# A long convolution's second transform step: from three rounded products on the whole array to fp32 products on its quarters

## The chip, the core and the metric

The kernel runs on one core of one Trainium2 chip. The metric is the device time of one execution in microseconds (us), and less is better. TensorE is PE in the profile, its weight loads are PEld, VectorE is DVE, ScalarE is ACT, GpSimd is POOL, and SP is SyncE, which here only issues DMAs.

## What is computed

One encoder block over 2048 tokens of 1024 channels, all in fp32. Cut to what matters:

```python
u = rmsnorm(x, norm_g);  p = einsum('bld,de->ble', u, w_in)          # 56 column blocks of 128
c_val, c_gate, c_z, hy_p, hy_z = split(p)
a = depthwise_conv(c_val * sigmoid(c_gate), 31 taps); a = silu(group_layernorm(a)) * silu(c_z)
x0, x1, v = split(depthwise_conv(hy_p, 3 taps))
k = filters(2L long)                                                  # a small MLP of positions
y = irfft(rfft(v * x1, 2L) * rfft(k, 2L), 2L)[:L] + (v * x1) * skip
y = group_rmsnorm(y * x0) * silu(hy_z)
out = rmsnorm(x + einsum('blm,md->bld', concat([a, y]), w_out), final_g)
```

## The kernel before

The program has five stretches. First the input's norm and some projections (0 to 100 us of the span) and the filters. Then, to 1500 us, the in-projections, with the convolution's taps on DVE beside them; each group of 128 channels of `a` is stored to the DRAM tensor `MX`, and the first step of the Fourier transform (`stage1`) stores signal and filter spectra to `AU` and `AK`. Third comes the **pair stage** (1500 to 1830 us), which the change rewrites. The last is the **epilogue** (to the end): for each of 16 blocks of 128 tokens `before` transforms back (products `Y`, transposes `T`, sums `vp`, rows `R`) and norms, and `after` multiplies by the second half of `w_out`. Between the two lies the **hand-over**.

The transform's second step works on 32 pairs of frequencies. A pair has 128 rows (2 frequencies, real and imaginary part, 32 places) of 1024 channels. Four products with 128x128 matrices `g` are needed: the signal's spectrum (`forward`), the filter's real and imaginary part (`product`, tiles `kr` and `ki`), and the way back (`inverse`). The two frequencies don't mix, so half of each matrix is zero. TensorE takes fp32r operands, which are rounded, in one instruction for 512 columns. To keep fp32's accuracy `parts` splits every operand on ACT and DVE into a rounded and a rest part, and `three` (L835 to L838) makes three products of them for each half of the channels. In every fifth pair (`DUP`) `product` makes one product less and copies instead.

`conf_step` is the first half of the out-projection, which needs `MX` alone: 16 blocks in two halves each, a half being 8 steps of 3 products (L781 to L783). 16 steps stand ahead of the pair stage, 176 are handed out within it (`some`, `CF`), the last 64 come behind it (`for _ in conf`). The Tile scheduler is free to order every engine's instructions. Tile `o` has one PSUM bank. `wo_split` (L490, L491) scales and splits the second half of `w_out`, into the tiles of the first, once `conf` is done with them.

`fetched` loads a block's gates `x0` and `hz` and the rows `v` (`long<-VD`) that `inverse` has stored to `VD`; a block's `v` has rows of all 32 pairs.

Of the kernel before, what the change touches and what calls it, by code (L numbers as in the profile page):

```python
# [18 lines left out]
P = 128  # L19
L = 2048  # L20
# [13 lines left out]
PITCH = (N2 + 1) * D  # L34
TWO_PI_INV = float(np.float32(1.0 / (2.0 * math.pi)))
# [9 lines left out]
DUP = 5  # L45
CF0 = 16
CF = 176
# [20 lines left out]
def _constants():  # L68
# [28 lines left out]
    st2 = np.zeros((NPAIR, P, 8, P), f32)  # L97
    n2 = np.arange(N2)[:, None]
    k2 = np.arange(N2)[None, :]
    for p in range(NPAIR):  # L100
        m = np.zeros((2, 2, N2, 2, 2, N2))
        for l in range(2):
            kk = l * 32 + p
            g = np.exp(-1j * np.pi * ((2 * kk + 1) * n2 / 4096.0 + k2 * n2 / 16.0))
            m[0, l, :, 0, l, :] = g.real
            m[1, l, :, 0, l, :] = -g.imag
            m[0, l, :, 1, l, :] = g.imag
            m[1, l, :, 1, l, :] = g.real
        m = m.transpose(2, 0, 1, 3, 4, 5).reshape(P, P)
        re, im = m[:, :64], m[:, 64:]  # L110
        for j, x in enumerate((m, m.T, np.concatenate([re, re], axis=1), np.concatenate([-im, im], axis=1))):
            st2[p, :, 2 * j], st2[p, :, 2 * j + 1] = _split(np.ascontiguousarray(x).astype(f32))
# [58 lines left out]
def hybrid_kernel(ctx: ExitStack, tc: tile.TileContext, A, out):  # L171
# [10 lines left out]
    MX = dram.tile([NG, P, L], F32, name="MX")  # L182
# [315 lines left out]
    with ExitStack() as c0:  # L498
# [78 lines left out]
        def conf_tail(i, acc, r, some):  # L577
# [12 lines left out]
            nc.sync.dma_start(MX[i], acc)  # L590
# [150 lines left out]
        def mixed(i, pool, bufs=1):  # L741

            mr = pool.tile([P, KT, P], F32, name="mr", bufs=bufs)
            nc.sync.dma_start(mr, MX[:, :, i * P:(i + 1) * P].rearrange("k p t -> p k t"))
            mh = pool.tile([P, KT, P], F32R, name="mh")
            nc.scalar.activation(mh, mr, AF.Copy)
            ml = pool.tile([P, KT, P], F32R, name="ml")
# [42 lines left out]
    pso = ctx.enter_context(tc.tile_pool(name="psO", bufs=1, space=PSUM, reuse_waits="tile"))  # L790
# [29 lines left out]

    def conf_to(n):

        while held[0] < min(n, 2 * KT * (L // P)):
            next(conf)

    with ExitStack() as c0:
# [8 lines left out]
        def three(o, g, j, hi, lo, cs):  # L835
            mm(o, g[:, j], hi[:, cs], start=True, stop=False)
            mm(o, g[:, j], lo[:, cs], start=False, stop=False)
            mm(o, g[:, j + 1], hi[:, cs], start=False, stop=True)  # L838

        seen = [0]  # L840

        def some():
            seen[0] += 1
            conf_to(CF0 + CF * seen[0] // (6 * NPAIR))

        HALF = [slice(c * TC, (c + 1) * TC) for c in range(2)]

        def load_pair(p):
            g = f1.tile([P, 8, P], F32R, name="g", bufs=4)
            nc.gpsimd.dma_start(g, A["c_st2"][p])  # L850
# [3 lines left out]
            nc.sync.dma_start(ak, gather(AK, p))  # L854
            return g, au, ak

        def parts(x, name, bufs, pool):
            if pool is None:
                both = long(F32R)
                h, l = both[:, :D], both[:, D:]  # L860
            else:
                h, l = (pool.tile([P, D], F32R, name=name + w, bufs=bufs) for w in "hl")
            nc.scalar.activation(h, x, AF.Copy)
            nc.vector.tensor_sub(l, x, h.bitcast(F32))
# [195 lines left out]
```

## Time and profile before

| what | value |
|---|---|
| median of 3 runs | 2160.95 us (2158.88 to 2162.77) |
| the profiled execution | 2159.41 us, its span 2157.7 us |
| PE busy | 2076.8 us, 96% of the span |
| DVE, ACT busy | 1581.6 us (73%), 1127.2 us (52%) |
| granted TensorE clock, mean | 0.99 |

Shares are means over the whole span. A matmul's duration in the trace holds its way through the array, so consecutive ones overlap; what one costs in a row of many is the distance between their starts. A `x` count in a row of the trace counts instructions; an fp32 product of TensorE is two of them, an fp32r product is one.

### The profile page before, as it was taken

The page shows a single profiled execution, that of the slowest core. Times are in us where ns is not written, and L with a number is a line of the kernel's source. Part 1 is how long each engine was busy: PE and PEld are TensorE (multiplying, and loading weights), DVE is VectorE, ACT ScalarE, POOL GpSimd, SP SyncE. Part 2 cuts the span into 40 slices and gives each one's busy share as a digit, 9 for nine tenths or more (in the row PEclk, how much of TensorE's full clock was granted, in tenths as well). Part 3 has the DMA queues.
Part 4 walks back from the last instruction along what each step waited for, and adds up shares of the span by engine and source line. Part 5 has one row for each costly group of instructions (what it writes and reads, how often), then busy time and mean ns, then how long its engine had stood idle before and what let it go on. Part 6 is the DMA issues. An engine that isn't in the chain of part 4 may idle for free. (4 is left out here: it accounts for less than half of the span.)

```text
span 2157.7 us, 23506 instructions
## 1 busy us (share of the span) xinstructions
PE 2076.8 (96%) x9076; PEld 1617.5 (75%) x9076; DVE 1581.6 (73%) x1519; ACT 1127.2 (52%) x1663; POOL 25.3 (1%) x52
## 2 busy tenths in 40 slices
PE   6999999999999999999999999999999999999998
PEld 5677788887887887877878878777777776666666
DVE  5687639498597695994994976986787886375664
ACT  6488712333434433433344344447898997365662
POOL 0000000000000000000000000001000000000000
PEclk9999999999999999999999999999999999999999
DMA  8433311112112202212121121127877786776652
GB/s 311 157 116 147 140 37 52 67 59 74 45 69 78 78 25 74 78 35 92 60 67 51 65 77 54 59 79 251 298 267 259 262 277 229 254 205 185 186 159 66
DMA packets 157104, 277.34 MB, mean 129 GB/s; under 512 B 11062, under 2 KB 93366, under 8 KB 151872
## 3 DMA queue, kind: packets, MB, share of 16 engines
q1 hardware_dynamic: 151008, 253.82, 35.8%
q0 software_dynamic: 5984, 22.02, 3.3%
q8 instruction: 71, 1.16, 0.2%
q14 instruction: 41, 0.34, 0.0%
HBM read 175.14 MB, written 100.66 MB: 128 GB/s over the span
## 5 line engine op out<-in xcount | busy, mean ns | idle before, releaser
L235 PE MATMUL mm<-uh,wh 128*128 128x512 f32 x1792 | 709.8, 397 | 6.8 <-ACT wh L226 3.5
L236 PE MATMUL mm<-ul,wh 128*128 128x512 f32 x1792 | 705.4, 394 | 1.6 <-DVE ul L296 1.6
L237 PE MATMUL mm<-uh,wl 128*128 128x512 f32 x1792 | 705.4, 394 | 0.3 <-DVE wl L228 0.3
L541 DVE SCALAR_TENSOR_TENSOR long<-apad,small,long 128x2048 f32<-128x2048 f32 x240 | 562.7, 2344 | 9.2 <-ACT long L538 6.7
L235 PEld LDWEIGHTS mm<-uh,wh 128*128 128x128 f32 x1792 | 340.3, 190 | 88.9 <-DVE apad L533 5.9
L236 PEld LDWEIGHTS mm<-ul,wh 128*128 128x128 f32 x1792 | 340.2, 190 | 77.7 <-DVE ul L296 3.6
L237 PEld LDWEIGHTS mm<-uh,wl 128*128 128x128 f32 x1792 | 339.8, 190 | 74.8 <-issue 1.6
L608 ACT ACTIVATE ppad<-mm 128x512 f32<-128x512 f32 x96 | 57.3, 597 | 224.6 <-PE mm L237 203.0
L783 PE MATMUL o<-wo,ml 128*128 128x512 f32 x384 | 152.2, 396 | 0.0
L781 PE MATMUL o<-wo,mh 128*128 128x512 f32 x384 | 152.0, 396 | 0.0
L782 PE MATMUL o<-wo,mh 128*128 128x512 f32 x384 | 151.9, 396 | 0.0
L226 ACT ACTIVATE wh<-wr 128x1024 fp32r<-128x1024 f32 x56 | 59.3, 1060 | 154.7 <-PE mm L236 147.4
L533 DVE TENSOR_TENSOR apad<-mm,apad 128x512 f32<-128x512 f32 x32 | 22.1, 692 | 154.7 <-PE mm L237 154.7
L228 DVE TENSOR_TENSOR wl<-wr,wh 128x1024 fp32r<-128x1024 f32 x56 | 68.3, 1220 | 53.7 <-ACT wh L226 52.7
L664 ACT ACTIVATE t<-aux 64x512 fp32r<-64x512 f32 x64 | 37.8, 594 | 103.5 <-PE aux L662 103.5
L782 PEld LDWEIGHTS o<-wo,mh 128*128 128x128 f32 x384 | 72.2, 188 | 18.9 <-issue 3.3
L783 PEld LDWEIGHTS o<-wo,ml 128*128 128x128 f32 x384 | 72.2, 188 | 18.1 <-issue 2.9
L781 PEld LDWEIGHTS o<-wo,mh 128*128 128x128 f32 x384 | 72.2, 188 | 17.0 <-issue 1.2
L564 ACT ACTIVATE long<-aux 128x512 f32<-128x512 f32 x32 | 19.0, 594 | 101.3 <-PE aux L563 101.3
L619 ACT ACTIVATE long<-ppad,small 128x512 f32<-128x512 f32 x64 | 68.8, 1076 | 1.9
L621 DVE SCALAR_TENSOR_TENSOR long<-ppad,small,long 128x512 f32<-128x512 f32 x64 | 66.8, 1046 | 0.7 <-ACT long L619 0.5
L681 ACT ACTIVATE t<-aux 128x512 f32<-128x512 f32 x64 | 37.7, 590 | 55.6 <-PE aux L679 55.4
(217 smaller groups left out, 3116.8 us busy)
## 6 DMA issues: line engine op xcount, KB each, us to landing
wr<-in_w_in_dram SPq DMA_DIRECT2D x56, 512.0 KB, 3.6
AK<-ak SPq DMA_DIRECT2D x64, 256.0 KB, 2.0
AU<-t SPq DMA_DIRECT2D x64, 256.0 KB, 2.3
au<-AU SPq DMA_DIRECT2D x32, 512.0 KB, 4.6
g<-in_c_st_dram POOLq DMA_DIRECT2D x32, 512.0 KB, 5.9
ak<-AK SPq DMA_DIRECT2D x32, 512.0 KB, 5.3
VD<-vs SPq DMA_DIRECT2D x32, 512.0 KB, 5.3
long<-VD SPq DMA_DIRECT2D x16, 1024.0 KB, 5.3
```

The lines of the kernel that those rows point to most:

```text
L226: nc.scalar.activation(wh, wr, AF.Copy)
L228: nc.vector.tensor_sub(wl, wr, wh.bitcast(F32))
L235: mm(pt, wh[:, k], uh[t][:, k], start=(k == 0), stop=False)
L236: mm(pt, wh[:, k], ul[t][:, k], start=False, stop=False)
L237: mm(pt, wl[:, k], uh[t][:, k], start=False, stop=(k == KT - 1))
L541: nc.vector.scalar_tensor_tensor(acc, apad[:, j:j + L], sm("dw_w", i * CK + j), acc, op0=OP.mult, op1=OP.add)
L608: nc.scalar.activation(ppad[:, 1 + t * TC:1 + (t + 1) * TC], pt, AF.Copy)
L619: nc.scalar.activation(co, v(ppad[:, a + 1:a + 1 + n]), AF.Identity, bias=sm("sh_b", j), scale=sm("sh_w", 3 * j + 1))
L621: nc.vector.scalar_tensor_tensor(co, v(ppad[:, a:a + n]), sm("sh_w", 3 * j), co, op0=OP.mult, op1=OP.add)
L781: mm(o, mh[:, k], wh[:, cs], start=(k == 0), stop=False)
L782: mm(o, mh[:, k], wl[:, cs], start=False, stop=False)
L783: mm(o, ml[:, k], wh[:, cs], start=False, stop=(k == KT - 1))
```

## The change

The 128x128 matrices become 64x64 ones without the zero blocks, in fp32 and unsplit. `quads` makes one of the four products of a pair: four `mm` calls, one for each frequency and each half of the channels, each on 64 rows and 64 columns of the array, that is on a quarter; the two row halves write different halves (PSUM banks) of the output tile. `parts` and the `DUP` branch go. ACT copies the spectrum out in one 128x1024 piece and swaps real and imaginary rows by four copies of 32 rows. `g` becomes 128x288 and is loaded by SP instead of POOL; `au`, `ak` and `vs` move in two DMAs of 64 rows each.

PE and SP now follow the program's order in the pair stage (`manual_schedule`): all four products of a round stand together, then 7 or 8 steps of `conf`. A block of `conf` is loaded and split one block ahead (`prepare`), and `o` has two banks. 8 steps of `conf` stand ahead of the stage and 8 behind the last `inverse`. `MX` is laid out by blocks of tokens, so that its load has 4 KB in a row and its store 512 B. Four row blocks of `w_out` and the first block's gates are loaded within the stage, and the first `wo_split` writes a tile of its own. `xr<-PT` moves from SP to POOL.

```diff
+KR, UU, KI, BACK = 0, N2, 3 * N2, 5 * N2
+NG2 = BACK + P
-DUP = 5
-CF0 = 16
-CF = 176
+CF0 = 8
+CF7 = 14
+CFY = 6
...
-    MX = dram.tile([NG, P, L], F32, name="MX")
+    MX = dram.tile([L // P, P, NG, P], F32, name="MX")
...
-            nc.sync.dma_start(MX[i], acc)
+            nc.sync.dma_start(MX[:, :, i].rearrange("b p t -> p b t"), acc.rearrange("p (b t) -> p b t", t=P))
...
-            nc.sync.dma_start(mr, MX[:, :, i * P:(i + 1) * P].rearrange("k p t -> p k t"))
-            mh = pool.tile([P, KT, P], F32R, name="mh")
+            nc.sync.dma_start(mr, MX[i])
+            mh = pool.tile([P, KT, P], F32R, name="mh", bufs=bufs)
...
-    pso = ctx.enter_context(tc.tile_pool(name="psO", bufs=1, space=PSUM, reuse_waits="tile"))
+    pso = ctx.enter_context(tc.tile_pool(name="psO", bufs=2, space=PSUM, reuse_waits="tile"))
...
+    def prepare(i):
+        parts = mixed(i, f1, 2) if i else first.pop()
+        xr = row()
+        nc.sync.dma_start(xr, A["x"][i * P:(i + 1) * P])
+        state[i] = (xr, *parts)
-        if c == 0:
-            mh, ml = mixed(i, io, 2) if i else first.pop()
-            xr = row()
-            nc.sync.dma_start(xr, A["x"][i * P:(i + 1) * P])
-            state[i] = (xr, mh, ml)
+        if c == 0 and i + 1 < L // P:
+            prepare(i + 1)
...
-        def gather(src, p):
-            return bass.AP(tensor=src.tensor, offset=src.offset + p * PITCH,
-                           ap=[[D, N2], [32 * PITCH, 4], [1, D]])
-        seen = [0]
-        def some():
-            seen[0] += 1
-            conf_to(CF0 + CF * seen[0] // (6 * NPAIR))
+        def gather(src, p, l):
+            return bass.AP(tensor=src.tensor, offset=src.offset + (32 * l + p) * PITCH,
+                           ap=[[D, N2], [64 * PITCH, 2], [1, D]])
...
-            g = f1.tile([P, 8, P], F32R, name="g", bufs=4)
-            nc.gpsimd.dma_start(g, A["c_st2"][p])
-            au = f1.tile([P, D], F32, name="au", bufs=2)
-            nc.sync.dma_start(au, gather(AU, p))
-            ak = f1.tile([P, D], F32, name="ak", bufs=2)
...
+            g = f1.tile([P, NG2], F32, name="g", bufs=4)
+            nc.sync.dma_start(g, A["c_st2"][p])
+            both = []
+            for name, src, bufs in (("au", AU, 2), ("ak", AK, 3)):
+                x = f1.tile([P, D], F32, name=name, bufs=bufs)
+                for l in range(2):
+                    nc.sync.dma_start(x[rows2(l)], gather(src, p, l))
+                both.append(x)
+            return g, *both
+        def quads(name, bufs, g, at, x, back=False):
+            o = ps.tile([P, D], F32, name=name, bufs=bufs)
+            for l in range(2):
+                for c in range(2):
+                    j = at + 64 * l * back
+                    i, k = (c, l) if back else (l, c)
+                    mm(o[rows2(k), HALF[i]], g[rows2(i), j:j + 64], x[rows2(i), HALF[k]], start=True, stop=True)
+            return o
+        def spectrum(g, au, ak):
             both = long()
             us, uw = both[:, :D], both[:, D:]
...
+            nc.scalar.activation(us, quads("u", 1, g, UU, au), AF.Copy)
+            for q in range(4):
+                nc.scalar.activation(uw[32 * q:32 * (q + 1)], us[32 * (q ^ 1):32 * (q ^ 1) + 32], AF.Copy)
+            return g, us, uw, ak
+        def product(g, us, uw, ak):
+            k = [quads("k", 2, g, at, ak) for at in (KR, KI)]
+            for x, y in zip((us, uw), k):
+                nc.vector.tensor_mul(x, x, y)
+            y = fp.tile([P, D], F32, name="y", bufs=2)
+            nc.vector.tensor_add(y, us, uw)
+            return g, y
...
+            nc.scalar.activation(vs, quads("u", 1, g, BACK, y, back=True), AF.Copy)
+            for l in range(2):
+                nc.sync.dma_start(gather(VD, p, l), vs[rows2(l)])
+        with tc.manual_schedule(engines={mybir.EngineType.PE, mybir.EngineType.SP}):
+            loads = {p: load_pair(p) for p in range(2)}
+            prepare(0)
+            conf_to(CF0)
+            spec = spectrum(*loads.pop(0))
+            y = None
+            for p in range(NPAIR):
+                if p == 0:
+                    done, y = None, product(*spec)
+                    spec = spectrum(*loads.pop(1))
+                    loads[2] = load_pair(2)
+                else:
+                    now = spec
+                    if p + 1 < NPAIR:
+                        spec = spectrum(*loads.pop(p + 1))
+                    done, y = y, product(*now)
+                if p + 3 < NPAIR:
+                    loads[p + 3] = load_pair(p + 3)
+                if done is not None:
+                    inverse(p - 1, *done)
+                if p == 3:
+                    nc.sync.dma_start(HZ[NG - 1], hz)
+                if p == NPAIR - 4:
+                    for k in range(4):
+                        wo_load(1, k)
+                    ahead = gates(0, io)
+                conf_to(held[0] + (CFY if p == NPAIR - 1 else 7 if p < CF7 else 8))
+            inverse(NPAIR - 1, *y)
+            for _ in conf:
+                pass
+        wo_split(1, 0, io.tile([P, 2 * D], F32R, name="wo0"))
...
+        def fetched(b, ahead=None):
+            x0, hz = ahead or gates(b, ep)
...
-                nc.sync.dma_start(pt[js], src)
+                nc.gpsimd.dma_start(pt[js], src)
...
-        rest = [fetched(0)]
-        for k in range(4):
-            wo_load(1, k)
-        rest.append(fetched(1))
-        for _ in conf:
-            pass
-        for k, make in enumerate([apad_tile, ppad_tile]):
-            wo_split(1, k, make(F32R))
-        for k in range(2, KT):
+        rest = [fetched(0, ahead), fetched(1)]
+        for k in range(1, KT):
             if k >= 4:
                 wo_load(1, k)
-            wo_split(1, k, wo_tile(k))
+            wo_split(1, k, apad_tile(F32R) if k == 1 else ppad_tile(F32R) if k == 2 else wo_tile(k - 1))
```

On PE, in the pair stage (tiles `uv` belong to `forward` or `inverse`), this is a piece of before:

```order
L836 MATMUL kr<-akh,g 128x512
L837 MATMUL kr<-akl,g 128x512
L838 MATMUL kr<-akh,g 128x512
L837 MATMUL uv<-aul,g 128x512
L838 MATMUL uv<-auh,g 128x512
L837 MATMUL uv<-aul,g 128x512
L838 MATMUL uv<-auh,g 128x512
L836 MATMUL uv<-long,g 128x512
L837 MATMUL uv<-long,g 128x512
L838 MATMUL uv<-long,g 128x512
L836 MATMUL ki<-akh,g 128x512
L781 MATMUL o<-apad,mh 128x512
```

and this a whole round of the change, with the ends of the `conf` steps around it:

```order
L788 MATMUL o<-wo_10090,mh 128x512
L789 MATMUL o<-wo_10090,ml 128x512
L875 MATMUL u<-au,g 64x512 x4
L875 MATMUL k<-ak,g 64x512 x8
L875 MATMUL u<-y,g 64x512 x4
L787 MATMUL o<-wo_10125,mh 128x512
L788 MATMUL o<-wo_10125,mh 128x512
```

The sixteen products of a round (`x4`, `x8`, `x4`) stand in one run; the last round's way back, alone, is followed by 24 products of `conf` and then by the epilogue. On ACT two rounds of the change read:

```order
L882 ACTIVATE long<-u 128x1024
L884 ACTIVATE long<-long 32x1024 x2
L752 ACTIVATE mh<-mr 128x1024
L884 ACTIVATE long<-long 32x1024 x2
L897 ACTIVATE vs<-u 128x1024
L882 ACTIVATE long<-u 128x1024
L884 ACTIVATE long<-long 32x1024 x4
L897 ACTIVATE vs<-u 128x1024
```

Tile `u` has one buffer, so the second `u` of a round waits for `long<-u`, and the next round's first for `vs<-u`. On SP the hand-over of before reads (`t` are rows of `w_out`, `x_...` and `hz` gates):

```order
L913 DMA VD<-vs 32x4x1024
L744 DMA mr<-MX 128x8x128
L804 DMA xr<-in_x_dram 128x1024
L952 DMA x_12947<-X_60 128x8x128
L954 DMA hz<-HZ 128x8x128
L956 DMA long<-VD 128x2048
```

and that of the change:

```order
L899 DMA VD<-vs 32x2x1024 x2
L487 DMA t<-in_w_out_dram 128x512
L899 DMA VD<-vs 32x2x1024 x2
L487 DMA t<-in_w_out_dram 128x512 x3
L824 DMA PT<-xr 128x1024
L950 DMA long<-VD 128x2048
```

The gates are gone from ahead of the first `long<-VD`; three loads of `w_out` and the last store of `PT` stand there instead.

## Rows read from the trace of the kernel before

**Rows 1.** The page: busy time by engine; DMA share in 40 slices of the span

```profile
PE 2076.8 (96%) x9076; PEld 1617.5 (75%) x9076; DVE 1581.6 (73%) x1519; ACT 1127.2 (52%) x1663; POOL 25.3 (1%) x52
DMA  8433311112112202212121121127877786776652
```

**Rows 2.** Three stretches; us, busy (instructions) of PE, PEld, DVE, ACT, POOL, clock, DMA, GB/s

```profile
1500.40:1829.30 328.90, 316.99 (x1310) 239.78 (x1308) 255.89 (x239) 283.06 (x412) 14.86 (x28) 1.00 0.79 269
1829.30:1901.70 72.40, 64.81 (x279) 41.90 (x277) 32.82 (x43) 33.63 (x49) 0.00 (x0) 1.00 0.81 259
1901.70:2157.70 256.00, 247.44 (x1134) 169.77 (x1132) 148.16 (x196) 134.09 (x227) 0.00 (x0) 0.99 0.56 154
```

**Rows 3.** Timeline of PE: start, duration; first and last of 23 products in a row

```profile
1838.04 0.39 PE L782 MATMUL o<-apad,mh 128*128 128x512 f32 x1
...
1843.15 0.40 PE L783 MATMUL o<-wo,ml 128*128 128x512 f32 x1
```

**Rows 4.** Line L836, first of `three`, in the pair stage: PE, PEld, clock, DMA, GB/s

```profile
1500.00:1831.00 331.00, 99.45 (x244) 45.48 (x244) 1.00 0.79 268
```

**Rows 5.** Waits of PE in the pair stage: us in total, times, longest

```profile
PE uv L836 <- ACT long L878: 3.8, 12, 0.8
PE kr L836 <- ACT t L892: 2.6, 4, 1.3
```

**Rows 6.** Timeline of PE around four fp32 products on a quarter of the columns each

```profile
419.96 1.07 PE L569 MATMUL vp<-long,ones_g 128*32 128x512 f32 x8
420.96 0.50 PE L235 MATMUL mm<-uh,wh 128*128 128x512 f32 x1
```

**Rows 7.** Timeline of PE around four fp32 products on half of the columns each

```profile
1945.78 0.39 PE L783 MATMUL o<-wo,ml 128*128 128x512 f32 x1
1946.11 1.94 PE L969 MATMUL Y<-long,winv 128*64 128x512 f32 x8
1947.97 0.50 PE L781 MATMUL o<-apad,mh 128*128 128x512 f32 x1
1948.31 0.39 PE L782 MATMUL o<-apad,mh 128*128 128x512 f32 x1
```

**Rows 8.** Weight loads of `Y`: busy us, mean ns of one, idle before

```profile
L969 PEld LDWEIGHTS Y<-long,winv 128*64 128x64 f32 x128 | 8.6, 135 | 14.7 <-issue 11.9 <-ACT y L971 1.1 <-DMA xr<-PT 0.4
```

**Rows 9.** ACT and DVE in the pair stage, by line: busy us, mean ns of one

```profile
L877 ACT ACTIVATE long<-uv 64x512 f32<-64x512 f32 x64 | 38.2, 596 | 1.1
L876 ACT ACTIVATE long<-uv 128x512 f32<-128x512 f32 x64 | 38.1, 595 | 8.5 <-PE uv L838 6.3 <-DVE long L864 0.8
L863 ACT ACTIVATE auh<-au 128x1024 fp32r<-128x1024 f32 x32 | 33.8, 1057 | 8.4 <-PE uv L838 7.8 <-ACT akh L863 0.3
L901 DVE TENSOR_TENSOR long<-long,ki 128x1024 f32<-128x1024 f32 x26 | 31.7, 1220 | 1.1 <-PE ki L838 1.1
```

**Rows 10.** The page's DMA issues: KB each, us from issue to landing

```profile
au<-AU SPq DMA_DIRECT2D x32, 512.0 KB, 4.6
```

**Rows 11.** Timeline of the hand-over, SP's queue and PE: start, duration

```profile
1835.39 3.08 SPq L956 DMA_DIRECT2D long<-VD  x1
1828.99 0.40 PE L838 MATMUL uv<-long,g 128*128 128x512 f32 x1
1845.11 1.07 PE L969 MATMUL Y<-long,winv 128*64 128x512 f32 x2
1901.66 0.78 PE L781 MATMUL o<-apad,mh 128*128 128x512 f32 x1
```

**Rows 12.** Two operations of the epilogue: busy us, mean ns of one

```profile
L986 DVE RECIPROCAL r<-r 128x256 f32<-128x256 f32 x16 | 28.0, 1749 | 2.9 <-ACT r L985 2.7
L996 ACT ACTIVATE mh<-m 128x1024 fp32r<-128x1024 f32 x16 | 16.9, 1053 | 23.9 <-PE o L782 17.3 <-DVE m L994 6.5
```

**Rows 13.** Line L969 in the hand-over, and the clock behind it (columns as in rows 2)

```profile
1845.00:1901.60 56.60, 11.62 (x36) 2.23 (x36) 0.99 0.76 244
1901.00:1905.00 4.00, 3.98 (x15) 2.37 (x15) 3.38 (x5) 2.40 (x4) 0.00 (x0) 0.57 1.04 240
```

More of the change, by code (lines that the diff above doesn't have):

```diff
@@ L95, in _constants @@
     st1 = np.stack([x for m in (s1u, s1k, s1k0) for x in _split(m.astype(f32))], axis=1)
-    st2 = np.zeros((NPAIR, P, 8, P), f32)
+    st2 = np.zeros((NPAIR, P, NG2), f32)
     n2 = np.arange(N2)[:, None]
@@ L100, in _constants @@
     for p in range(NPAIR):
-        m = np.zeros((2, 2, N2, 2, 2, N2))
+        fw = np.zeros((2, N2, 2, 5, N2))
+        bw = np.zeros((2, 2, N2, 2, N2, 2))
         for l in range(2):
@@ L104, in _constants @@
             g = np.exp(-1j * np.pi * ((2 * kk + 1) * n2 / 4096.0 + k2 * n2 / 16.0))
[L105 to L112, printed above, removed]
+            re = np.stack([g.real, -g.imag], axis=1)
+            im = np.stack([g.imag, g.real], axis=1)
+            for b, x in enumerate((re, re, im, -im, im)):
+                fw[l, :, :, b] = x
+            for h in range(2):
+                bw[h, 0, :, l] = re.transpose(2, 0, 1)
+                bw[h, 1, :, l] = im.transpose(2, 0, 1)
+        st2[p] = np.concatenate([fw.reshape(P, 5 * N2), bw.reshape(P, P)], axis=1)
     a = np.pi * (2 * np.arange(64)[:, None] + 1) * np.arange(64)[None, :] / 128.0
@@ L819, in hybrid_kernel, with gates @@
     conf = conf_steps()
+    def gates(b, pool):
+        x0 = pool.tile([P, NG, P], F32, name="x0")
+        nc.sync.dma_start(x0, X0[:, :, b * P:(b + 1) * P].rearrange("k p t -> p k t"))
+        hz = pool.tile([P, NG, P], F32, name="hz")
+        nc.sync.dma_start(hz, HZ[:, :, b * P:(b + 1) * P].rearrange("k p t -> p k t"))
+        return x0, hz
     def conf_to(n):
@@ L829, in hybrid_kernel @@
         ps = c0.enter_context(tc.tile_pool(name="psB", bufs=1, space=PSUM, reuse_waits="tile"))
-        def gather(src, p):
-            return bass.AP(tensor=src.tensor, offset=src.offset + p * PITCH,
-                           ap=[[D, N2], [32 * PITCH, 4], [1, D]])
[L835 to L838, printed above, removed]
@@ L857, in parts @@
[L857 to L864, printed above, removed]
-            return h, l
-        def both_parts(g, au, ak):
-            return g, parts(au, "au", 1, f1), parts(ak, "ak", 2, fp)
@@ L906, in inverse @@
-        def inverse(p, g, yh, yl):
-            vs = fp.tile([P, D], F32, name="vs", bufs=2)
-            for cs in HALF:
-                V = ps.tile([P, TC], F32, name="uv", bufs=3)
-                three(V, g, 2, yh, yl, cs)
-                nc.scalar.activation(vs[:, cs], V, AF.Copy)
-                some()
-            nc.sync.dma_start(gather(VD, p), vs)
-        conf_to(CF0)
-        loads = {p: load_pair(p) for p in range(2)}
-        nc.sync.dma_start(HZ[NG - 1], hz)
-        split = both_parts(*loads.pop(0))
@@ L919, in hybrid_kernel @@
-        spec = forward(*split)
-        split = both_parts(*loads.pop(1))
-        loads[2] = load_pair(2)
-        y = None
-        for p in range(NPAIR):
-            done = y
-            y = product(p, *spec)
-            if p + 1 < NPAIR:
-                spec = forward(*split)
-            if done is not None:
-                inverse(p - 1, *done)
-            if p + 2 < NPAIR:
-                split = both_parts(*loads.pop(p + 2))
-            if p + 3 < NPAIR:
-                loads[p + 3] = load_pair(p + 3)
@@ L934, in hybrid_kernel @@
-        inverse(NPAIR - 1, *y)
+            nc.scalar.activation(us, quads("u", 1, g, UU, au), AF.Copy)
[9 more added lines that the diff above has]
+            return g, y
@@ new lines, in inverse @@
+        def inverse(p, g, y):
+            vs = fp.tile([P, D], F32, name="vs", bufs=2)
+            nc.scalar.activation(vs, quads("u", 1, g, BACK, y, back=True), AF.Copy)
[31 more added lines that the diff above has]
+                pass
@@ L1005, in after @@
             for c, cs in enumerate(halves):
-                o = (ps if c else pso).tile([P, TC], F32, name="o")
+                o = pso.tile([P, TC], F32, name="o")
                 for _ in outproj(o, mh, ml, cs):
```

43 lines of the change are left out of this document (3 added, 40 removed).

## Prediction

> **What bounds the kernel now.** The page comes first [rows 1]: PE is busy 96% of the span, DVE 73%, ACT 52%, and the DMA engines stand at 7 to 8 tenths in the slices of the pair stage. PE therefore sets the time nearly everywhere, and a change pays where it takes work or gaps from PE. The windows show where [rows 2]: from 1500.4 to the last `inverse` at 1829.3 us PE started 1310 instructions; ACT was busy 283 of 329 us there, so it is close behind. What a product of the split kind costs is read from 23 starts in a row [rows 3]: (1843.15 - 1838.04) / 22 = 0.232 us. 1310 of them take 304 us, so 25 us of the 329 are gaps. The longest entries in the list of waits, 3.8 and 2.6 us, are on ACT's copies [rows 5]; most of the rest lies within overlapping durations, where the trace names nobody.
>
> **The products of the transform.** Line L836 ran 244 times in the stage [rows 4], L837 and L838 as often: 3 x 244 = 732 products x 0.232 = 169.8 us. All go. In their place stand 32 rounds of four `quads`, each of four fp32 products of 512 columns on a quarter of the array (32 x 4 x 4 = 512 products, 1024 instructions, so that the page's 9076 become 9368). What one `quads` costs hangs on how many quarters run at once. The trace has two relatives. Four fp32 products on a quarter of the columns each, 8 instructions, take 1.07 us from the first start to the last end, and the next matmul starts 1.00 us after the first [rows 6]: all four ran together, two instructions deep. Four on half of the columns each take 1.94 us, and the next starts 1.86 us after the first [rows 7]: two ran together, four deep. The difference, (1.86 - 1.00) / 2 = 0.43 us, is one such step. So the columns divide freely. That row halves do, no row shows: the nearest are full columns' worth of streams in [rows 6], where four different streams entered the array at once, while here there are two for each row half. Bounds for a `quads`: 2 steps = 0.86 us if the quarters run together, 4 steps = 1.72 if row halves take turns, 8 steps = 3.44 if nothing overlaps. I take 0.86, since rows of both kinds show the array dividing in as many parts as it is given, and the two row halves here write different banks.
>
> Going in and out of such a run costs a little [rows 7]: 0.33 us from the start of the last full product to the first `Y` where 0.232 is usual, 1.86 against 4 x 0.43 = 1.72 within, and 0.34 for the first full product after it: 0.10 + 0.14 + 0.11 = 0.35 us. It is paid once a round, as all sixteen products stand together. A round costs 4 x 0.86 + 0.35 = 3.8 us, 32 rounds 121 us: **49 us less on PE**.
>
> The Trainium skill ("TensorE: Matmul & The Clock Gate", Part 3, "The mechanism" and "What overlaps and what doesn't") says that a weight load overlaps with running matmuls only where the row group differs. Within a round every step needs weights for the same rows as the step before. The loads of `Y` take 135 ns each [rows 8] and are likewise for the same rows, and they did not show: [rows 7] leave 0.14 us over the four steps in all. By the rule each of 8 steps would be 0.135 longer, 8 x 32 x 0.135 = 35 us in all, an estimate; the trace decides for none. The same part ("Measured speedup vs the span model") gives 3.07 for four row tiles side by side in place of 4; by it a `quads` would be 3.44 / 3.07 = 1.12 us and the rounds 33 us longer, an estimate too. Both stand below as one rival, worked out as a mechanism of this kernel.
>
> **The gaps in the stage.** `parts` goes, three splits for each pair, 1.06 us on ACT [rows 9] and 1.22 on DVE each. ACT per round: `long<-u`, four copies of 32 rows and `vs<-u`, each 1024 columns, so about 1.06 us whatever the rows (64 and 128 rows both cost 0.6 for 512 columns in [rows 9]), and half of a split of `mr`: 6.5 x 1.06 = 6.9 us. A round on PE is 3.8 + 24 x 0.232 = 9.4 us, with 21 products 8.7. As `u` has one buffer there is a loop through ACT: first `quads` 0.86 and some 0.3 until ACT starts, `long<-u` 1.06, four copies 4.2, at times `mh` 1.06, `vs<-u` 1.06: 8.5 us at most. It fits, with 0.2 to 0.9 us to spare, and `long<-u` ends 2.3 us into the round, before the third `quads` ends at 2.7. DVE needs 3 x 1.22 + 0.6 + 0.7 = 5 us. Loads are issued two rounds ahead, some 15 us, and land in about 5 [rows 10]. DMA: 32 x (0.15 + 3 x 0.52) + 46 x 0.52 + 4 = 83 MB, which over 300 us is 277 GB/s; [rows 2] have 269 at a share of 0.79. It is tight but has room. I take 6 us of gaps for 25 now, **19 us less**; bounds 0 and 32 (1 us a round).
>
> **The hand-over.** The last `inverse` now starts its last product at 1829.0, `long<-VD` is issued at 1835.4, `Y` starts at 1845.1 and the first product of the epilogue's out-projection at 1901.7 [rows 11]. Between 1829.3 and 1901.7 PE started 279 instructions [rows 2], 36 of them `Y` [rows 13]; some 195 are `conf`. After the change only 24 are left there: 171 are done earlier, within the stage, and cover nothing here. So the last `inverse` comes at 1500.4 + (768 - 24) x 0.232 + 121 + 6 = 1800. From there: `v` must make its way out and in, 1845.1 - 1829.0 = 16 us as before (the gates no longer stand ahead of it, but three loads of `w_out` and a store do). Of these 5.6 are covered by `conf`; the splits of `w_out` on ACT and DVE fall into the rest. Then the chain from `Y` to the first `mh`, an estimate by the pieces' sizes: on PE the four products 1.9 [rows 7] and transposes, sums and `R` some 1.6; on ACT and DVE five pieces of 512 columns at 0.6 to 0.7, 3.2 [rows 9]; four of 256 columns at about 0.45, 1.8; the reciprocal 1.75 and `mh` 1.05 [rows 12]. That is 11.3 us, with a dozen handings-on of 0.1 to 0.2 us 13 to 14. The first out-projection product stands at 1800 + 16 + 14 + 1 = 1831 instead of 1901.7: 71 us earlier. But less of the epilogue is done by then: the program's order has 12 `Y` products, before there were 18 [rows 13], and ten transposes fewer: 3 + 1 + 0.5 = 4.5 us to be made up. PE sits idle for some 10 us on `v`. After the idle stretch ahead of 1901 the granted clock was 0.57 for 4 us [rows 13], that is, mostly 1.2 instead of 2.4 GHz; I add 1.5 us for slow products in the chain. Sum: -71 + 4.5 + 1.5 = **-65 us**. The same by parts: -49 - 19, and +3 for the hand-over.
>
> The epilogue's other edits I cost at nothing: `xr<-PT` on POOL leaves SP's queue, and PE was busy 247 of 256 us there [rows 2], so no load sets its pace. If POOL were late with them, `after` would wait at its add, a block later. The stores of `MX` in 512-byte pieces lie where the DMA share is 1 to 2 tenths [rows 1].
>
> **The number.** The profiled execution took 2159.4 us for a span of 2157.7. 2157.7 - 65 = 2093, with 1.7 around it 2094; the median of the runs is 1.5 above that execution, so 2095 us. 0.2% (4 us) is about what a measurement can tell from no change.
>
> **Rivals.**
> 1. *Row halves take turns.* For: no row shows them together. Against: [rows 6, 7] for columns. A `quads` is 1.72 us, a round 7.2; 32 x 3.44 = 110 us more: 2205 us, slower. It decides from a round of 3.8 + 65 / 32 = 5.8 us on.
> 2. *Something is exposed in each round*: weight loads, 8 x 0.135 = 1.1 us a round [rows 8], or the loop through ACT, if a copy of 32 rows takes 1.3 us (9.5 us for the loop against 8.7 to 9.4, some 0.5 us a round). 16 to 35 us: 2111 to 2130.
> 3. *DMA holds the stage back.* At the 269 GB/s of [rows 2] 83 MB take 309 us, 9 more than I have: 2104. Against: the packets of `MX` are larger now.
> 4. *The hand-over has no cover.* If `v` needs 5 us more behind the loads of `w_out`, and PE's order holds back `Y` or `R`: 2103. If it is quick and the gaps vanish (-6, -8): 2081; with rounds of 3.44 us, 2070.
>
> **Chances.** The forecast with rivals 3 and 4, 2080 to 2112: 0.60. Rival 2, 2112 to 2135: 0.15. Rival 1: 0.13. Quicker than 2080: 0.10. About no change, as a mixture of 1 and 2: 0.02. From 2070 to 2130 holds 0.8. Faster 0.85, the same 0.02, slower 0.13.
>
> **What would show it.** In the timeline of a round: eight groups of four starts 0.43 us apart, 3.8 us from `conf` to `conf`; if row halves take turns, sixteen groups of two. Then PE's waits in the stage: on `u` for ACT none over 0.5 us. The last `inverse` near 1800, `Y` 16 us later, out-projection from 1831, and 262 us from there to the end. I am wrong above all if a round is not 3.8 us, next if `u` waits for ACT.

## The result and the profile after

The changed kernel takes 2091.24 us (median of 4 runs, 2088.11 to 2094.68) against 2160.86 before (4 runs, 2158.88 to 2162.77): a ratio of 0.968, 95% interval 0.966 to 0.970. The forecast was 2095. The profiled execution took 2088.11 us for a span of 2086.3.

The page answers to [rows 1]: PE is still busy 96%, with the 9368 instructions that were counted out. What is new is the DMA row, 9 tenths throughout the pair stage.

```profile
PE 2006.1 (96%) x9368; PEld 1517.2 (73%) x9368; DVE 1468.1 (70%) x1411; ACT 1057.0 (51%) x1455; POOL 24.6 (1%) x52
DMA  8523412121221211212122212122899999877652
```

The windows of the pair stage, the hand-over and the epilogue (columns as in [rows 2]):

```profile
1500.10:1801.60 301.50, 296.58 (x1768) 173.79 (x1766) 154.47 (x144) 218.99 (x210) 0.00 (x0) 0.99 0.96 276
1801.60:1837.50 35.90, 22.00 (x80) 9.24 (x76) 18.05 (x24) 20.34 (x31) 3.07 (x6) 0.81 0.97 278
1837.50:2086.30 248.80, 240.58 (x1165) 169.22 (x1164) 150.42 (x200) 141.36 (x237) 13.23 (x26) 0.99 0.58 170
```

The stage is 27 us shorter although 171 more products of `conf` lie in it, and the hand-over has shrunk: from the last `inverse` to the first out-projection product of the epilogue (1840.2) it is 39 us instead of 72, and from there to the end 246 instead of 256. One round in the timeline of PE (start, duration):

```profile
1603.63 0.40 PE L789 MATMUL o<-wo,ml 128*128 128x512 f32 x1
1603.96 1.09 PE L875 MATMUL u<-au,g 64*64 64x512 f32 x8
1604.87 1.90 PE L875 MATMUL k<-ak,g 64*64 64x512 f32 x16
1606.58 1.04 PE L875 MATMUL u<-y,g 64*64 64x512 f32 x8
1607.55 0.50 PE L787 MATMUL o<-wo,mh 128*128 128x512 f32 x1
1607.89 0.39 PE L788 MATMUL o<-wo,mh 128*128 128x512 f32 x1
```

Read the distances between starts. The 16 instructions of `k` (two `quads`; a step is four instructions, one on each quarter) take 1606.58 - 1604.87 = 1.71 us, four steps of 0.43: all four quarters run at once. From the last `conf` product to the second one after the run it is 4.26 us; less 2 x 0.232 that is 3.80 us for a round's `quads`, the number of the forecast. After the first three, the rounds start 8.67 us apart with 21 products of `conf` (two of them 8.9 and 9.1), and 9.37 with 24, from 1630 to 1780 without exception.

PE's waits from 1490 to 1850 us (total, times, longest):

```profile
PE Y L963 <- DMA long<-VD: 11.9, 3, 7.4
PE u L875 <- ACT long L882: 2.2, 1, 2.2
PE o L787 <- ACT mh L752: 1.8, 1, 1.8
```

Within the stage there are two worth the name: `u` ahead of the first `inverse`, and `o` for `mh` near 1788 us, after which the clock fell to half for 3.4 us. The large one is in the hand-over, which the timeline shows; first SP's queue, then PE:

```profile
1802.97 1.16 SPq L899 DMA_DIRECT2D VD<-vs  x2
1808.76 0.36 SPq L950 DMA_DIRECT2D long<-VD  x1
1811.45 3.30 SPq L950 DMA_DIRECT2D long<-VD  x1
1816.22 9.64 SPq L834 DMA_DIRECT2D hz<-HZ  x1
1825.91 4.64 SPq L950 DMA_DIRECT2D long<-VD  x1
...
1814.95 3.47 PE L963 MATMUL Y<-long,winv 128*64 128x512 f32 x6 [7.39 <-DMA long<-VD]
1825.91 1.94 PE L963 MATMUL Y<-long,winv 128*64 128x512 f32 x2 [3.62 <-DMA long<-VD]
1836.86 1.04 PE L963 MATMUL Y<-long,winv 128*64 128x512 f32 x2 [0.91 <-DMA long<-VD]
1840.21 0.50 PE L787 MATMUL o<-wo,mh 128*128 128x512 f32 x1
```

The first `v` is there 13.8 us after the last product of the last `inverse` has started (1801.2). But in PE's order `Y` of the second and third block stand ahead of the first block's out-projection, and their `v` come late. The second block's was issued at 1811.45 and had landed only when `Y` started at 1825.91. Its packets of 8 KB moved from 1819.1 to 1824.7, after those of the gates issued ahead of it (1813.5 to 1818.2), with the DMA engines full:

```profile
1815.00:1825.90 10.90, 6.22 (x20) 1.90 (x21) 2.61 (x3) 3.29 (x5) 1.17 (x3) 0.81 1.08 286
```

The third block's was issued only at 1825.91, as one issue of `hz<-HZ` held SP's queue for 9.64 us before it. Behind the second block's `Y` stood the last four `vp` instructions of the first block, whose operand ACT had done at 1823.1: they ran at 1827.77. The out-projection starts at 1840.2.

### The profile page after: what moved, and what is told of

It is laid out like the page before. It is cut to its first block, busy times and chain, and to the rows that moved or that the text cites. A ratio compares the mean times of both kernels' runs of the same rounds, so it can differ in the third digit from the quotient of the medians.

```text
span 2086.3 us, 23788 instructions
## 1 busy us (share of the span) xinstructions
PE 2006.1 (96%) x9368; PEld 1517.2 (73%) x9368; DVE 1468.1 (70%) x1411; ACT 1057.0 (51%) x1455; POOL 24.6 (1%) x52
## 4 chain that ended last, share of the span: by engine, by line
PE 73%; DVE 17%; DMA 3%; issue 3%; ACT 3%; SPq 2%; DVEq 0%; ACTq 0%
PE mm L241 14%; PE mm L242 14%; PE mm L243 14%; DVE long L547 7%; PE o L787 5%; PE o L789 5%; PE o L788 5%; PE u L875 2%; PE k L875 2%; DVE long L628 2%; DVE long L627 2%; PE Y L963 1%; DVE t L671 1%; PE op L412 1%; PE op L411 1%
## 5 line engine op out<-in xcount | busy, mean ns | idle before, releaser
L787 PE MATMUL o<-wo,mh 128*128 128x512 f32 x384 | 156.9, 409 | 0.0
L788 PE MATMUL o<-wo,mh 128*128 128x512 f32 x384 | 151.6, 395 | 0.0
L890 DVE TENSOR_TENSOR long<-long,k 128x1024 f32<-128x1024 f32 x64 | 75.6, 1218 | 95.6 <-PE k L875 83.6
L884 ACT ACTIVATE long<-long 32x1024 f32<-32x1024 f32 x128 | 135.3, 1057 | 2.3
L234 DVE TENSOR_TENSOR wl<-wr,wh 128x1024 fp32r<-128x1024 f32 x56 | 68.5, 1224 | 54.0 <-ACT wh L232 53.1
```

Source lines behind the costliest of these rows:

```text
L234: nc.vector.tensor_sub(wl, wr, wh.bitcast(F32))
L787: mm(o, mh[:, k], wh[:, cs], start=(k == 0), stop=False)
L788: mm(o, mh[:, k], wl[:, cs], start=False, stop=False)
L884: nc.scalar.activation(uw[32 * q:32 * (q + 1)], us[32 * (q ^ 1):32 * (q ^ 1) + 32], AF.Copy)
L890: nc.vector.tensor_mul(x, x, y)
```

## The experiments

### What the quarters are worth: products on the whole array, still in fp32

```diff
-            for l in range(2):
-                for c in range(2):
-                    j = at + 64 * l * back
-                    i, k = (c, l) if back else (l, c)
-                    mm(o[rows2(k), HALF[i]], g[rows2(i), j:j + 64], x[rows2(i), HALF[k]], start=True, stop=True)
+            for k in range(2):
+                mm(o[:, HALF[k]], g[:, at:at + P], x[:, HALF[k]], start=True, stop=True)
```

The columns of `g` that it multiplies by are not the right ones; order, loads and sizes of the rest are kept.

> The change, but each of the four products of a round is taken on the whole array: one fp32 product of 128 rows and 128 columns for each half of the channels, with columns of the matrix tile that are not the right ones, so the values are not the transform's. My theory (PE sets the pace of the stage, and four quarters at once are what made the products cheap): 4 steps of 0.43 us for each of the four in place of 2, a round 3.75 to 7.2 us, 32 x 3.44 = 110 us more, 2201 us, the DMA share of the stage falling from 0.96 to about 0.7. Rival (the gain came from the freed ACT and DVE and from the order, and PE has slack in a round): under 60 us more, under 2150 us.

2187.11 us (one run). Rounds start 11.74 and 12.46 us apart, 3.07 to 3.09 more than after the change, and PE waits for nothing within them:

```profile
1612.78 1.88 PE L872 MATMUL u<-au,g 128*128 128x512 f32 x4
1614.50 3.60 PE L872 MATMUL k<-ak,g 128*128 128x512 f32 x8
1617.93 1.88 PE L872 MATMUL u<-y,g 128*128 128x512 f32 x4
```

Eight instructions of `k` take 1617.93 - 1614.50 = 3.43 us, 0.43 each: as long as a step of four quarters. So a quarter costs as much as the whole array and four run in that time, which halves the run from 6.88 to 3.44. The 3.08 are 3.44 less the 0.35 that going in and out of the quarters cost by the forecast. Without the quarters the change would have made the kernel 26 us slower.

### Is there a loop through ACT?

The prediction had a loop: `u` has one buffer, so the next `forward` waits until ACT has done `long<-u`, four copies, sometimes `mh`, and `vs<-u`. Two dead copies a round were added, first by the program's place only:

```diff
+            for _ in range(2):
+                nc.scalar.activation(us, us, AF.Copy)
             return g, us, uw, ak
```

> The change with two dead copies of 128x1024 more on ACT in each round, behind the four copies of 32 rows. My theory (tile u with its one buffer makes a loop through ACT that fits the round by 0.2 to 0.9 us): the loop grows from 7.4 or 8.5 us (the latter with a split of mr in it) to 9.5 or 10.6, rounds of 8.7 and 9.4 us grow to it, 14 rounds by some 1.4 us and 18 by some 0.7: about 32 us more, 2123 us, and PE's list of waits shows u waiting for vs<-u. Rival (ACT is busy 219 of 301 us in the stage, 287 with these, so they fit beside PE): at most 5 us more, 2088 to 2096.

2099.84 us (one run), 9 more. ACT was busy 245 of 260 us between 1520 and 1780, but from the fourth on the rounds stayed at 8.7 to 9.4 (the third took 17.3 where it had 11.3, which is 6 of the 9 us): the scheduler had placed most of the dead copies behind `vs<-u`, outside the loop. So this run did not test it. The second one writes them to `vs`, between the swap and the real copy, which overwrites them:

```diff
             vs = fp.tile([P, D], F32, name="vs", bufs=2)
+            if p < NPAIR - 2:
+                for _ in range(2):
+                    nc.scalar.activation(vs, spec[1], AF.Copy)
```

> Two dead 128x1024 copies a round on ACT, written to vs between the swap copies and vs<-u, so that they lie within the loop of u's one buffer (their result is overwritten). Theory of the loop: 0.86 + 0.3 + 1.06 + 4.2 + 2.1 + 1.06 = 9.6 us, and 1.06 more in each second round, against rounds of 8.7 and 9.4: +0.9 to 2.0 us in the 14 short rounds, +0.2 to 1.3 in the others, some 30 us in all: 2115 to 2130 us. Rival (only the sum of ACT's work counts, as where the same two copies stood mostly behind the loop and cost 9 us): 2095 to 2103 us.

2130.29 us (one run). The rounds alternate between 9.76 and 10.86 us, however many products of `conf` stand in them; the sum in the expectation had 9.6 and 10.7. PE's waits from 1500 to 1800, and ACT's timeline:

```profile
PE u L875 <- ACT vs L900: 29.9, 27, 2.1
```

```profile
1652.23 1.02 ACT L882 ACTIVATE long<-u 128x1024 f32<-128x1024 f32 x1 [1.21 <-PE u L875]
1653.28 3.19 ACT L884 ACTIVATE long<-long 32x1024 f32<-32x1024 f32 x3
1656.50 1.06 ACT L752 ACTIVATE mh<-mr 128x1024 fp32r<-128x1024 f32 x1
1657.59 1.06 ACT L884 ACTIVATE long<-long 32x1024 f32<-32x1024 f32 x1
1658.67 2.15 ACT L899 ACTIVATE vs<-long 128x1024 f32<-128x1024 f32 x2
1660.85 1.02 ACT L900 ACTIVATE vs<-u 128x1024 f32<-128x1024 f32 x1
```

The loop is real. It is not ACT's load that counts: here ACT was busy less than in the run before (226 of 260 us) and the time was 30 us longer. Less the 2.15 of the dead copies it takes 7.6 us, or 8.7 with `mh` in it, against rounds of 8.67: a short round of the change that has `mh` in its loop has no slack.

### More cover for the hand-over

`CF7 = 32` gives every round 7 steps instead of 7 or 8, so that some 25 steps of `conf` instead of 8 lie behind the last `inverse`, where PE stood idle.

```diff
-CF7 = 14
+CF7 = 32
```

> The change with 7 conf steps in every round but the last, so that 25 steps instead of 8 stand behind the last inverse. Theory A (PE's idle time on v in the hand-over, 7.4 us ahead of the first Y, and the half clock behind it can be covered): the last inverse ends 12 us earlier, the first Y starts right behind conf, 6 to 12 us less, 2079 to 2085. Theory B (the splits of w_out wait for the end of conf and hold back the out-projection, or rounds of 8.7 us outrun the DMA engines, whose share is 0.96 already): 2088 to 2098, with gaps in the rounds or ahead of the out-projection.

2101.43 us (2100.57 to 2101.97), ratio 0.972 [0.971, 0.974]: 10 us slower than the change. The last `inverse` is at 1800.3 where it was at 1801.2, though 12 us of work have left the stage. After the first three, four rounds take 10.0 to 13.6 us, the others 8.7 to 8.9; PE waits 7.8 us for `mh` and 2.6 for `ml`, five times each. One of them, in PE's timeline and by windows:

```profile
1743.87 0.50 PE L787 MATMUL o<-apad,mh 128*128 128x512 f32 x1 [2.34 <-ACT mh L752]
```

```profile
1744.00:1746.00 2.00, 1.48 (x6) 0.92 (x7) 1.67 (x2) 0.73 (x1) 0.00 (x0) 1.00 1.07 242
1746.00:1748.00 2.00, 2.00 (x7) 1.59 (x6) 0.00 (x0) 0.00 (x0) 0.00 (x0) 0.53 1.00 268
```

`mh` stands behind the four copies on ACT, PE waits 2.34 us for it, and then the granted clock is 0.53, that is, mostly 1.2 instead of 2.4 GHz.

That the stage gives nothing back is one half of the loss; the other half lies behind it, from PE's timeline:

```profile
1823.93 0.66 PE L968 MATMUL T<-ident,y 128*128 128x128 f32 x4 [3.50 <-ACT y L965]
1842.98 1.97 PE L963 MATMUL Y<-long,winv 128*64 128x512 f32 x2 [7.97 <-DMA long<-VD]
1853.06 0.40 PE L787 MATMUL o<-wo,mh 128*128 128x512 f32 x1
```

The first `Y` now follows `conf` without a gap, at 1818.49. But the splits of `w_out` wait for the end of `conf` and keep ACT until 1823.4, so `T` waits for `y`, and `v` of the third block, issued at 1825.6, is awaited for 8 us. From the first `Y` to the out-projection it is 34.6 us instead of 25.3. So the second theory of the expectation holds in its first part. I first put the time lost in the stage down to the DMA engines, which were at 0.95; the next runs took that apart.

### Are the DMA engines the bound of the stage?

In the first try the constants were permuted so that a pair's rows could move in one DMA each:

```diff
-            return bass.AP(tensor=src.tensor, offset=src.offset + (32 * l + p) * PITCH,
-                           ap=[[D, N2], [64 * PITCH, 2], [1, D]])
+            return bass.AP(tensor=src.tensor, offset=src.offset + p * PITCH,
+                           ap=[[32 * PITCH, 4], [D, N2], [1, D]])
...
-                for l in range(2):
-                    nc.sync.dma_start(x[rows2(l)], gather(src, p, l))
+                nc.sync.dma_start(x, gather(src, p, 0))
```

> The rows of a pair are ordered differently in DRAM (the constants are permuted to match), so that au, ak and vs move in one DMA of 128 rows each instead of two of 64. Same bytes. Theory A (DMAs of 64 rows keep the DMA engines longer for the same bytes): the DMA share of the pair stage falls from 0.96 to about 0.80 at the same 275 GB/s, the landings of au and ak from 7 to about 5 us; since PE sets the stage, only the hand-over gains: 2083 to 2090 us. Theory B (the share is high because the queues are filled two rounds ahead): share above 0.9, time 2088 to 2095 us.

> The same, and CF7 = 32, which moves 16 to 18 half-block steps from the stage behind the last inverse, where PE stood idle. With 64-row DMAs this cost 10 us because the DMA engines became the bound of the stage. Theory A: now they don't: rounds of 8.7 us throughout, the last inverse near 1788, 12 us less idling behind it: 2078 to 2085 us. Theory B: the DMA engines bind as before, rounds of 9 to 13 us, 2098 to 2104 us.

2382.81 and 2390.93 us, ratios 1.104 [1.102, 1.106] and 1.107 [1.105, 1.109]: a miss that I had not foreseen. The DMA rows of 1600 to 1800 us in the first of the two (40 slices):

```profile
DMA  2232276222325223822223293222327722232592
GB/s 106 97 124 107 104 257 176 107 97 102 124 105 204 108 105 123 231 105 105 99 104 130 120 294 121 105 102 103 125 108 240 188 106 100 104 127 104 194 244 104
```

In most slices the 16 engines stood at 2 tenths and moved about 105 GB/s; where other loads ran it was up to 294. From 1636 to 1650 the share is 0.26, about what four busy engines of sixteen make. The Trainium skill ("DMA: Bandwidth & Descriptors", "Rules for kernel authors") says that the slowest dimension of the address pattern sets how many engines share a DMA; it is 4 here and 32 before and after the change, and these rows agree with it.

In the second try the first step writes the rows of a pair one behind the other, so that the DMA's outermost dimension is 128:

```diff
-    AU = dram.tile([P, N2 + 1, D], F32, name="AU")
+    AU = dram.tile([P, N2, D], F32, name="AU")
...
-                for l in range(2):
-                    nc.sync.dma_start(x[rows2(l)], gather(src, p, l))
+                nc.sync.dma_start(x, src[4 * p:4 * p + 4].rearrange("k n d -> (k n) d"))
```

> The rows of a pair stand in DRAM one behind the other (the columns of the first step's matrix and the rows of g are permuted to match, AU and AK lose their padding), so that au and ak move in one DMA of 128 rows each, whose outermost dimension is 128; vs stays at two of 64 rows. Theory A (DMAs of 64 rows keep the DMA engines longer for the same bytes): the DMA share of the pair stage falls from 0.96 to about 0.85 at 275 GB/s, au and ak land in about 5 us instead of 7; PE sets the stage, so 2084 to 2092 us. Theory B (the share is high because the queues are filled two rounds ahead): share above 0.92, 2088 to 2096 us.

> The same, and CF7 = 32, which leaves some 17 half-block steps more behind the last inverse, where PE stood idle. Alone this cost 10 us, and I read the DMA engines as the bound of the stage then. If A holds: rounds of 8.7 us throughout, the last inverse near 1788, 8 to 12 us less idling behind it: 2076 to 2085 us. If B holds: rounds of 9 to 13 us, 2096 to 2104 us.

2096.57 us (2096.02 to 2099.02), ratio 0.970 [0.969, 0.972], and with `CF7 = 32` 2102.76 (2100.69 to 2104.01), 0.973 [0.971, 0.975]. First the window of 1540 to 1780 us of the first of them, then its DMA issues there:

```profile
1540.00:1780.00 240.00, 236.60 (x1426) 138.57 (x1425) 124.01 (x116) 174.99 (x169) 0.00 (x0) 1.00 0.85 274
```

```profile
au<-AU SPq DMA_DIRECT2D x26, 512.0 KB, 4.4
ak<-AK SPq DMA_DIRECT2D x26, 512.0 KB, 5.6
```

The share is 0.85 at 274 GB/s instead of 0.97 at 277 for the same stretch after the change, and `au` lands in 4.4 us instead of 6.9. So two DMAs of 64 scattered rows each keep the engines longer than one of 128 rows that stand together in DRAM. The run changes both, the number of rows and their place; that the number does it is not shown by it, though the share of 0.79 at 269 GB/s in [rows 2], with 128 scattered rows in one DMA, speaks for it. But nothing is gained: the stage alone, from the first `quads` to the last, takes 303.2 us where the change has 295.9, and with `CF7 = 32`, engines at 0.84 and 12 us less work, still 296.5. So the DMA engines' share was not the bound. `CF7 = 32` costs 6 us here; as before they are lost behind the stage, where it is 53.1 us from the last `inverse` to the out-projection instead of 41.3. What held the stage is in ACT's waits from 1500 to 1800 us, and in the timeline of ACT and PE at one of its rounds (both with `CF7 = 14`):

```profile
ACT mh L753 <- DMA mr<-MX: 10.6, 8, 2.5
ACT hz L976 <- DMA hz<-HZ: 4.7, 1, 4.7
```

```profile
1533.46 1.06 ACT L753 ACTIVATE mh<-mr 128x1024 fp32r<-128x1024 f32 x1 [2.47 <-DMA mr<-MX]
1534.42 1.00 ACT L897 ACTIVATE vs<-u 128x1024 f32<-128x1024 f32 x1
...
1535.48 1.09 PE L875 MATMUL u<-au,g 64*64 64x512 f32 x8 [2.22 <-ACT vs L897]
```

Here the scheduler has put `mh` between the four copies and `vs<-u`, in the round in which `mr` is loaded (issued at 1525.66). ACT waits 2.47 us for the load within the loop, and PE 2.22 for ACT. After the change the same `mh` stands behind `vs<-u` and no one waits. The second line is the activation of the first block's gates, which stands ahead of `long<-u` at 1788.6: PE waits 3.3 us behind it, and 6.1 with `CF7 = 32`, where PE's waits for ACT's copies of `u` are 16.5 us in all. ACT's order is not written by hand, and in these rounds it decides.

### The layout of MX

As before the change, by channels; the rest as after.

> MX laid out by channels as before the change: its load in pieces of 512 bytes instead of 4 KB, its store in whole rows; the rest as after the change. Theory A (with the DMA engines at 0.96 the small pieces cost time in the stage): rounds rise above 9.4 us at places, 2096 to 2110 us. Theory B (prefetch hides it): 2088 to 2095 us.

2093.03 us (one run). The load in pieces of 512 bytes raises the packets between 1540 and 1780 us from 22364 to 33178 and the share from 0.97 to 0.99; the rounds stay at 8.67 and 9.37, only `Y` comes 15.2 us after the last `inverse` instead of 13.8. The new layout is worth 2 us, if anything.

### The written order of PE and SP

```diff
-        with tc.manual_schedule(engines={mybir.EngineType.PE, mybir.EngineType.SP}):
+        with ExitStack():
```

> The pair stage without the written order of PE and SP: the scheduler places the instructions. The products of the rounds then stand in 75 runs instead of 33, and 512 of them fill 148 steps of four instead of 128. Theory A (a run costs 0.35 us, a step of four two times 0.43 us, whether full or not): 42 x 0.35 + 20 x 0.86 = 32 us more: 2115 to 2130 us. Theory B (split runs hide the waits for ACT and cost little): 2085 to 2098 us.

2141.31 us (one run): the stage is 44 us longer, with PE busy 234 of the 240 us from 1540 to 1780. The order is worth that, more than the 32 us that runs and half-filled steps would make by the expectation's prices; waits for `mh` (3.5 us) and `u` (4.7 us) are some of the rest, and the remainder stays open.

### Why the epilogue became quicker

The prediction gave 262 us from the first out-projection product of the epilogue to the end; it took 246.1. A block, by DVE's first add on `o`, takes 15.45 us from the second on; before it took 16.4 over the first eight and 15.4 to 16.2 from then on. (The last two of each kernel are shorter, as they have no `Y` left beside them.) Waits don't explain it: 0.2 us in all before (1930 to 2110 us), none after (1860 to 2040). Two causes were tried. First, `xr<-PT` back on SP:

```diff
-                nc.gpsimd.dma_start(pt[js], src)
+                nc.sync.dma_start(pt[js], src)
```

> The change with xr<-PT back on SP's queue. The epilogue of the change is quicker than I had it: a block takes 15.45 us where it took about 16 before. Theory A (the PT loads stood in SP's order ahead of the gates and v of later blocks and held them up): the block goes back to about 16 us, 8 us more, about 2099. Theory B (it comes from the order of PE or from elsewhere): within 4 us of the change, 2087 to 2095, block 15.4 to 15.5 us.

2094.32 us (2093.35 to 2095.32), ratio 0.969 [0.968, 0.971]. The first four blocks take 16.4 us on the mean, later ones 15.47. It shifts the order on PE at the start; by the medians that is 3 us, and the two ranges overlap. Second, one bank of `o` for the epilogue, two in the pair stage:

```diff
-        o = pso.tile([P, TC], F32, name="o")
+        o = pso.tile([P, TC], F32, name=f"o{c}")
...
-                o = pso.tile([P, TC], F32, name="o")
+                o = pso.tile([P, TC], F32, name="o0")
```

(with `bufs=1` for the pool)

> The epilogue's out-projection uses one bank for o, as before the change; the pair stage keeps two. Theory A (the epilogue is 14 us quicker because o's second bank lets the scheduler place the column products together): the rest from the first out-projection product of the epilogue goes back from 246 to 254 to 260 us, 2096 to 2104 us. Theory B (it has nothing to do with o): 244 to 249 us, 2086 to 2094 us.

2116.48 us (one run): the blocks take 17.21 us and the rest 272.9, more than expected. Again PE waits for nothing. What differs is what stands next to what. The two groups that use a part of the array's columns, from the first out-projection product on: before, after, and with one bank.

```profile
L969 PE MATMUL Y<-long,winv 128*64 128x512 f32 x92 | 27.9, 608 | 0.0
L981 PE MATMUL vp<-sq,ones_g 128*32 128x256 f32 x112 | 15.6, 400 | 0.0
```

```profile
L963 PE MATMUL Y<-long,winv 128*64 128x512 f32 x110 | 27.1, 605 | 0.0
L975 PE MATMUL vp<-sq,ones_g 128*32 128x256 f32 x112 | 9.6, 391 | 0.0
```

```profile
L963 PE MATMUL Y<-long,winv 128*64 128x512 f32 x104 | 38.0, 611 | 0.0
L975 PE MATMUL vp<-sq,ones_g 128*32 128x256 f32 x104 | 16.3, 391 | 0.0
```

The mean of one is the same everywhere, but the busy time for so many (the first number, overlaps counted once) is 0.30, 0.25 and 0.37 us for an instruction of `Y`, and 0.14, 0.09 and 0.16 for one of `vp`. Eight `Y` in a row take 1.94 us (1946.88 in the timeline of after); as six and two, with transposes and `R` between them, 1.93 and 1.07 (1918.83 with one bank). With `vp` it is plainest, first after the change, then with one bank:

```profile
1953.76 0.64 PE L975 MATMUL vp<-sq,ones_g 128*32 128x256 f32 x8
```

```profile
1928.95 0.62 PE L975 MATMUL vp<-sq,ones_g 128*32 128x256 f32 x4
1931.11 0.63 PE L975 MATMUL vp<-sq,ones_g 128*32 128x256 f32 x4
```

Four instructions by themselves take as long as eight together. From before to after this makes 92 x 0.057 + 112 x 0.053 = 11 us, which is what the blocks gained (221.7 instead of 232.9 us from the first add to that of the last block). It is the order that counts and not the bank as such: before the change, on one bank, three blocks in a row have all eight `Y` and all eight `vp` together, and they take 15.42 to 15.47 us as after it; the blocks ahead of them with split groups take up to 19.8. That no other difference of the orders has a part in it isn't shown.

## Why the prediction was right, and where it was not

- **The products of the transform** (-49 us): right in every part. 3.80 us a round, steps of 0.43, and with them 0.35 for going in and out, confirmed by the timeline or by the run on the whole array. Rival 1 (row halves take turns) would have shown steps of `k` twice as long.
- **Rival 2's weight loads**: within a `quads` every step loads weights for the rows that are running, 131 to 133 ns each, and the steps stay at 0.43 us. The Trainium skill's rule ("TensorE: Matmul & The Clock Gate", "What overlaps and what doesn't") by which such loads show is not what this trace has; nor does the 3.07 for four row tiles that the same page of the Trainium skill has ("Measured speedup vs the span model") carry over to these quarters: four of them take the 0.43 us of one instruction on the whole array.
- **The gaps in the stage** (6 us): 744 x 0.232 + 32 x 3.80 = 294.2 of the 301.1 us to the last `inverse`, so 6.9. It started at 1801.2 against 1800. That the loop through ACT "fits" was right for the order that ACT got, and by how little was shown with two dead copies.
- **The hand-over**: the first `Y` was 2 us quicker than the 16 forecast, but the out-projection came at 1840.2, not at 1831. The step that failed is "the chain from `Y` to the first `mh`", summed as if the first block had PE to itself: 25 us instead of 15. PE's order has `Y` of two more blocks ahead, whose `v` were late, the second on full DMA engines and the third behind the 9.64 us issue as well; the clock was at 0.75 to 0.81 of full speed; and on ACT a split of `w_out` (0.72 us) and a table load (1.28 us, `ACT_TABLE_LOAD` at 1829.22) stood between the sums and `r`, which the sum did not have. PE's order holding back `vp` and `R` is one half of rival 4; its other half, a late first `v`, did not come. Priced there at 8 us, the hand-over as a whole cost 8.
- **The epilogue's edits** ("cost at nothing"): wrong, on the other side: the rest from the out-projection took 246 us instead of 262. The blocks gained 11 of the 16, where the scheduler kept the groups of `Y` and `vp` together. The second bank of `o` was not among the edits that I weighed there; without it this program's groups fall apart, though before the change some blocks had them whole on one bank, and why the scheduler chooses as it does stays open. The other 5 are most of the 6 us that the sum added for work not yet done and for slow products: from the out-projection to the first add it took 10.7 us instead of 9.3, no more. The argument that PE was busy 247 of 256 us, hence nothing to gain, took busy time for work: PE's busy time is itself longer where such groups are split.
- **The sum**: +1 in the stage, +8 in the hand-over, -16 in the epilogue: -7, the span 2086.3 instead of 2093. That the forecast of 2095 is 4 us from the median is in part luck: two errors of opposite sign met.
- **DMA** (rival 3): bytes and rate as forecast (276 GB/s for 277), the room was not: 0.96 of the engines' time instead of some 0.8. With one DMA of 128 rows that stand together it was 0.84 to 0.85. In the stage it stayed hidden behind loads two rounds ahead; in the hand-over the full engines made the second block's `v` late.

No version here beats the change; what the runs point to as a reserve is ACT's order in the pair stage and the 25 us between the first `Y` and the out-projection, and neither was tried.

## What to carry to other kernels

Price a run of small products by the distance between starts in groups that already run side by side, and count how often the order goes in and out of such a group: here the written order, which keeps the groups whole, was worth 44 us in one stage (32 of them by those prices), and whole groups go with 11 us in another, where no wait showed it. Before work is moved to cover an idle stretch, look at both ends: the stage that it leaves may wait for another engine instead, and what waits for the end of that work (here the splits of `w_out`) comes later. And an engine's order that the scheduler sets can change with any edit; compare it on every engine, not only where the edit is.

## What the runs showed of the hardware that was not expected

- An fp32 instruction of 512 columns costs 0.43 us on a quarter of the array as on all of it (3.43 us for 8 on the whole, 1.71 for 16 on quarters).
- DMAs whose outermost dimension was 4 ran at about 105 GB/s with the engines at a share of 0.26; with 128 in the place of 4 the stage's loads moved 274 GB/s.
- One issue of a 512 KB load (`hz<-HZ`) held SP's queue for 9.64 us while the DMA engines were full (1.08); others of its kind took 0.4 to 1.4. Why is open.
- Two waits of PE of 2.34 and 0.53 us in one round were followed by a stretch at the lower clock (0.53), and the round was 4.9 us longer than its neighbours. Another round of the same run with 2.00 and 0.52 us of waiting kept the full clock (1.00 from 1767.2 to 1772) and was 3.1 us longer.
